# Forming the low parts of the first block's mixer weights with accumulating DMAs instead of VectorE subtractions

## The chip, the cores and the metric

The kernel runs on one core of a Trainium2 chip. The metric is the device time of one execution in microseconds (us). The kernel before takes 1753.9 us (median of three runs, 1749.92 to 1758.46).

## The reference

The reference is two transformer-like blocks on 512 tokens of width 1024, all in fp32. The first block (the one that the change touches) projects the modulated input `h` into its mixers and merges them:

```python
h = modulate(rmsnorm(x, norm1_g[i]), sh1, sc1)
q, k, v, hv, hx1, hx2, gna, ghy = jnp.split(h @ w_in[i], IN_SPLITS, axis=-1)
y_na = neighbourhood_attention(to_heads(q), to_heads(k), to_heads(v), to_heads(k_c), to_heads(v_c), na_rpb[i])
y_hy = hyena_mixer(hv, hx1, hx2, *hy_params)
x = x + g1 * gated_merge(gna, ghy, y_na, y_hy, w_na_o[i], w_hy_o[i], w_out[i])
```

`k_c` and `v_c` come from a second, 256-token context through `w_in`, the shift and scale `sh1`, `sc1` from a conditioning vector through `w_ada`, and the Hyena filters from a small network. Then come a SwiGLU layer, and the second block with three more mixers and a convolutional feed-forward layer. Nothing of these is changed.

## The kernel before

**How a product is computed.** Every large matrix product is done in three TensorE passes on the type fp32r, which holds a shortened fp32. A weight tile `w` is split into a high part `wh` (ScalarE's copy of `w` into fp32r, shown as CAST) and a low part `wl = w - wh` (VectorE's TENSOR_TENSOR, `lo`, line 778). `mm` (line 788) then adds `wh*xh + wh*xl + wl*xh` in one PSUM bank. The other operand `x` is split in the same way.

**How weights arrive.** `stream` (line 797) is a generator over weight groups of 128 x 1024 fp32 (512 KB, eight blocks of 128 x 128). For each it takes a buffer `raw`, loads it on SP's queue, takes `wh` and `wl`, and splits. The seven streams that the change touches are `w_hy` (12 groups, Hyena's input projection), `w_kvc` (4, the context's keys), `w_na` (12, attention's q, k and v), `w_gna` and `w_ghy` (8 each, the gates), `w_hyo` and `w_nao` (4 each, the output projections): 52 groups. All other streams, the modulation weights `w_ada` and the row-wise weights keep the subtraction.

**What sets the order.** No engine's order is written by hand. The program records every operation as a call, and `Trace.schedule` (line 542) simulates all engines with modelled durations and hand-over times (the tables `LAG`, `RELEASE` and the function `time`). It gives each engine the ready call of best rank, hands out SBUF space (48 segments named `pages`) and PSUM banks as it goes, and repeats forward and backward passes to improve the ranks (`plan`, line 691). `emit` (line 707) then issues the calls in the order of their planned starts from one line, 714; so every instruction of the trace carries that line, and tiles are told apart only by `pages`, `banks`, `small` or a name such as `mod`. Each engine works its own instructions strictly in this order and waits on semaphores. SP carries all DMAs of the kernel before; GpSimd (POOL) only clears padding.

**The start.** TensorE works first on the Hyena filters and on the modulation (`modulation_first`, line 1027: sixteen `w_ada` groups, each split and multiplied by the conditioning vector). Beside it VectorE and ScalarE compute the norm of `x`: squares, their sum, a reciprocal square root in a chain of small VectorE operations (tile `small`), a broadcast by TensorE, and then eight scaling operations that read `gs1` and eight that subtract the high part of `h` (they read `mod`). The first product of `h` with `w_hy` follows. From there on the filters, the context branch and the gates are woven between the products of the mixers.

Of the kernel before, what the change touches and what calls it, by code (L numbers as in the profile page):

```python
# [15 lines left out]
F32 = mybir.dt.float32  # L16
F32R = mybir.dt.float32r
I32 = mybir.dt.int32
BF16 = mybir.dt.bfloat16
AF = mybir.ActivationFunctionType  # L20
ALU = mybir.AluOpType
# [140 lines left out]
def layout(inp):  # L162
# [77 lines left out]

ENGINES = ("tensor", "vector", "scalar", "gpsimd", "sync")
PE, DVE, ACT, POOL, DMA = range(5)

LAG = (
    (0.0, 197.0, 197.0, 220.0, 1280.0),
    (152.0, 127.0, 128.0, 155.0, 1220.0),
    (108.0, 131.0, 150.0, 165.0, 1235.0),
    (75.0, 75.0, 75.0, 102.0, 1170.0),  # L250
    (1500.0, 2000.0, 1000.0, 1300.0, 2250.0),
)
APART = 0.7
ALONE = (DVE,)
DMA_START = 1700.0
RELEASE = 200.0, 150.0, 150.0, 100.0, 1200.0
TABLES = {AF.Silu: (0,), AF.Sin: (1, 0), AF.Exp: (2,), AF.Gelu_apprx_tanh: (3,)}
TABLE_LOAD = 1283.0
WEIGHTS = 13.3
# [203 lines left out]
class Trace:  # L463
    def __init__(self, nc, tc):
        self.nc, self.tc = nc, tc
        self.calls, self.lead, self.urgent = [], 0, False
        for i, name in enumerate(ENGINES):
            setattr(self, name, Engine(self, (i,)))
        self.either = Engine(self, (DVE, POOL))

    @contextmanager
# [6 lines left out]
    @staticmethod  # L478
    def time(engine, name, out, args, kw):

        n = out.free_size()
        if engine == PE:
            cols = args[1].ap.free_size()
            if name == "transpose":
                return max(2 * n / 2.4, 53)
            if args[1].ap.dtype == F32R:
                return max(n / 2.4 + WEIGHTS, cols / 1.2 + 5.0)
            return max(4 * n / 2.4 + 2.5, cols / 0.6 if n < 16 else cols / 0.3 if cols > 64 else 54)
        if engine == DVE:
            return (98 if name == "scalar_tensor_tensor" else 70) + 1.042 * n  # L490
        if engine == ACT:
            return 60 + 0.87 * n + (120 if name == "activation" and ("scale" in kw or "bias" in kw) else 0)
        if engine == POOL:
            return 150 + 2.1 * n
        return max(450.0, out.size() * 4 / 360.0)

    @staticmethod
    def shares_port(engine, name, reads, writes):
# [219 lines left out]
class Program:  # L718
# [75 lines left out]
        mm(out, wl, xh, start=False, stop=stop)  # L794
        self.pe += 3 * out.ap.free_size() / 2.4

    def stream(self, ap):

        for gi in range(ap.shape[0]):
            raw = self.u4()  # L800
            self.load(raw, ap[gi])
            wh, wl = self.u4(dt=F32R), self.u4(dt=F32R)
            self.split((wh, wl), raw)
            for j in range(8):
                yield wh[:, j * P : j * P + P], wl[:, j * P : j * P + P]

# [399 lines left out]
    def hyena(self):  # L1206
        nc, a = self.nc, self.a
        V = nc.vector
        blocks = self.stream(a["w_hy"])

        def conv_tile(m):
            ps = self.proj(blocks, self.h)
# [121 lines left out]
    def context(self):  # L1334

        nc = self.nc
        self.context_norm()
        yield
        blocks = self.stream(self.a["w_kvc"])
        self.kc, self.vc = [], []  # L1340
        for j in range(6):
            if j < 4:
                ps = self.proj(blocks, self.hc, 256)
            elif j == 4:
                out = self.proj_rows(self.a["w_vc"], self.hc)
            if j >= 4:
                t = self.u4(dt=F32R)
                self.vc.append(t)
                v, ps = t.rearrange("p (h z d) -> p h z d", z=2, d=64), out[j - 4].rearrange("p (h d) -> p h d", d=64)
                d = v[:, :, 0], v[:, :, 1]  # L1350
                nc.scalar.copy(d[0], ps)
                nc.vector.tensor_tensor(out=d[1], in0=ps, in1=d[0].bitcast(F32), op=ALU.subtract)
            else:
                self.kc.append(self.stacked_keys(ps, 256))
            yield
# [88 lines left out]
    def neighbourhood(self):  # L1444
        nc, a = self.nc, self.a
        V = nc.vector
        rope = self.u4()
        self.load(rope, a["rope1"])
        rc, rs = rope[:, :T], rope[:, T:]
        swap = [(i + 16) % 32 for i in range(32)]  # L1450
        blocks = self.stream(a["w_na"])
        self.y_na = []

        def rotate(x):
            sh, t1 = self.u2(), self.u2()
            V.stream_shuffle(sh, x, swap)
            nc.gpsimd.tensor_tensor(out=t1, in0=x, in1=rc, op=ALU.mult)
            V.tensor_tensor(out=sh, in0=sh, in1=rs, op=ALU.mult)
            V.tensor_tensor(out=t1, in0=t1, in1=sh, op=ALU.add)
            return t1  # L1460

        for hp in range(4):

            ps = self.proj(blocks, self.h)
            q = self.u2()
            nc.scalar.activation(q, ps, AF.Copy, scale=0.125)
            qp = self.stacked_queries(q)
            qr = self.stacked_queries(rotate(q))
            yield
            ps = self.proj(blocks, self.h)  # L1470
            k = self.u2()
            nc.scalar.copy(k, ps)
            kr = self.stacked_keys(rotate(k))
            yield
            ps = self.proj(blocks, self.h)
            v = self.u2()
            nc.scalar.copy(v, ps)
            vof = {}
            for off in ((0, 128, 256, 384), (64, 192, 320)):
                pt = self.psum("t")  # L1480
                n = len(off)
                for j, o in enumerate(off):
                    self.transpose(pt[:, j * P : j * P + P], v[:, o : o + P])
                t = self.u4(n * 256, F32R)
                to, ptv = t.rearrange("p (j h z d) -> p j h z d", h=2, z=2, d=64), pt[:, : n * P].rearrange("p (j h d) -> p j h d", h=2, d=64)
                for hd in range(2):
                    nc.scalar.copy(to[:, :, hd, 0], ptv[:, :, hd])
                    V.tensor_tensor(out=to[:, :, hd, 1], in0=ptv[:, :, hd], in1=to[:, :, hd, 0].bitcast(F32), op=ALU.subtract)
                vof.update((o, t[:, j * 256 : j * 256 + 256]) for j, o in enumerate(off))
            yield  # L1490
            o, sums = self.u2(), self.u0(8)
            for hd in range(2):
                bias = self.u4(768)
                self.load(bias, a["rpb"][2 * hp + hd])
                banks = []
                for b in range(4):
                    s = self.psum("s")
                    off = WIN_OFF[b]
                    kind = (0, 1, 1, 2)[b]
                    qsl = slice(b * P, b * P + P)  # L1500
                    self.scores(s[:, :256], hd, qr, qsl, kr, off)
                    self.scores(s[:, 256:], hd, qp, qsl, self.kc[hp], 0)
                    st = self.u0(6)
                    V.tensor_tensor_reduce(out=s[:, :256], in0=s[:, :256], in1=bias[:, kind * 256 : kind * 256 + 256], scale=1.0, scalar=-3e38, op0=ALU.add, op1=ALU.max, accum_out=st[:, 0:1])
                    V.reduce_max(out=st[:, 1:2], in_=s[:, 256:], axis=AX.X)
                    V.tensor_scalar(out=st[:, 2:3], in0=st[:, 0:1], scalar1=st[:, 1:2], scalar2=-1.0, op0=ALU.max, op1=ALU.mult)
                    pr = self.u2()
                    nc.scalar.activation(pr, s, AF.Exp, bias=st[:, 2:3], accum_out=sums[:, hd * 4 + b : hd * 4 + b + 1])
                    if b % 2 == 0:
                        banks.append(self.psum("o"))  # L1510
                    values = [vof[off + j * P][:, hd * P : hd * P + P] for j in range(2)]
                    values += [self.vc[j][:, (2 * hp + hd) * P : (2 * hp + hd) * P + P] for j in range(2)]
                    self.stacked_pv(banks[-1][:, b % 2 * 256 : b % 2 * 256 + 256], [pr[:, j * P : j * P + P] for j in range(4)], values)
                    yield
                self.summed_parts(o[hd * 64 : hd * 64 + 64], banks)
            d = self.over_sums(o, sums)
            self.y_na.append(d)
            yield
# [4 lines left out]

    def gate_na(self):

        blocks = self.stream(self.a["w_gna"])
        self.gna = self.scratch("gna")
        for m in range(KT):
            ps = self.proj(blocks, self.h)
# [5 lines left out]
    def branch_hy(self):  # L1535

        nc = self.nc
        gb, ob = self.stream(self.a["w_ghy"]), self.stream(self.a["w_hyo"])
        self.bhy = self.scratch("bhy")
        for m in range(0, KT, 2):  # L1540
            gs = []
# [11 lines left out]
    def merge1(self, mem):  # L1553
        nc, a = self.nc, self.a
        V = nc.vector
        ob = self.stream(a["w_nao"])
        nat = lambda x: x.rearrange("p (cb r c) -> p cb r c", r=8, cb=8)
        merged = []
        for m in range(KT):
            gb = self.u4()  # L1560
# [762 lines left out]
```

## Time and profile before

| | value |
|---|---|
| median of three runs | 1753.9 us |
| the profiled execution's own time | 1758.72 us |
| its span, first to last instruction | 1756.9 us |
| its mean granted TensorE clock | 0.993 of full speed |
| TensorE matmul busy | 1710.2 us, 97% |
| VectorE busy | 1194.7 us, 68% |
| ScalarE busy | 729.7 us, 42% |
| GpSimd busy | 29.2 us, 2% |
| DMA | 235.42 MB, mean 134 GB/s |

Busy time is what an engine spent in instructions that compute; waiting, semaphores and the issuing of DMAs are not in it. The granted clock is given as a share of full speed, 2.4 GHz; the lower of its two levels is 1.2 GHz, so 0.84 in a stretch says that about a third of that stretch ran at the lower level. The 40 slices of the page (44 us each) show how TensorE, VectorE and the DMA engines are loaded over the span: TensorE is below nine tenths in the first two slices alone, VectorE is at eight or nine tenths in the second to sixth, the tenth to thirteenth and the 28th to 31st.

### The profile page before, as it was taken

How to read it: one execution, taken by the hardware profiler on the slowest of the kernel's cores; microseconds unless marked ns; L12 is line 12 of the kernel's file. 1: busy time of each engine (PE TensorE's matmuls, PEld its weight loads, DVE VectorE, ACT ScalarE, POOL GpSimd, SP SyncE). 2: the span in 40 equal slices, each digit the busy share in tenths (PEclk: the TensorE clock that was granted, in tenths of full speed). 3: DMA queues.
4: the chain of work that ended last, by engine and by line, in shares of the span. 5: the costliest groups of instructions: out<-in, count | busy, mean ns of one | idle time of the engine just before them, and what ended most of it. 6: DMA issues, size and time to landing. Idle time of an engine off the chain costs nothing. (4 is left out here: it accounts for less than half of the span.)

```text
span 1756.9 us, 22940 instructions
## 1 busy us (share of the span) xinstructions
PE 1710.2 (97%) x8494; PEld 1416.4 (81%) x8494; DVE 1194.7 (68%) x2473; ACT 729.7 (42%) x1204; POOL 29.2 (2%) x69
## 2 busy tenths in 40 slices
PE   4799999999999999999999999999999999999999
PEld 3489988888888888888887887888877888888887
DVE  6999887759998266344377856659998635887520
ACT  5634345655554121233153431556564412454310
POOL 0000000000000000000000000010100000000000
PEclk9899999999999999999998999999999999999999
DMA  7644332427963324313254455412257221222420
GB/s 253 233 142 143 100 102 90 145 84 251 356 242 119 112 92 160 119 61 127 77 175 163 142 145 158 135 60 75 85 196 271 98 94 60 81 76 72 146 100 19
DMA packets 93662, 235.42 MB, mean 134 GB/s; under 512 B 18316, under 2 KB 26252, under 8 KB 93550
## 3 DMA queue, kind: packets, MB, share of 16 engines
q1 hardware_dynamic: 93550, 233.95, 39.2%
q8 instruction: 67, 1.10, 0.3%
q14 instruction: 45, 0.37, 0.1%
HBM read 206.91 MB, written 27.00 MB: 133 GB/s over the span
## 5 line engine op out<-in xcount | busy, mean ns | idle before, releaser
L714 PE MATMUL banks<-pages,pages 128*128 128x512 f32 (+5 forms) x7830 | 1663.5, 372 | 30.9 <-ACT pages L714 21.3
L714 PEld LDWEIGHTS banks<-pages,pages 128*128 128x128 f32 (+3 forms) x7830 | 1343.0, 185 | 305.8 <-ACT pages L714 25.3
L714 DVE TENSOR_TENSOR pages<-pages,pages 128x1024 fp32r<-128x1024 f32 (+12 forms) x747 | 616.7, 855 | 99.0 <-ACT pages L714 69.7
L714 ACT CAST pages<-pages 128x1024 fp32r<-128x1024 f32 (+4 forms) x471 | 396.9, 871 | 350.9 <-PE banks L714 111.6
L714 DVE TENSOR_TENSOR pages<-banks,pages 128x512 fp32r<-128x512 f32 (+7 forms) x219 | 111.8, 523 | 95.4 <-PE banks L714 73.4
L714 DVE TENSOR_TENSOR pages<-banks,R 128x512 f32<-128x512 f32 x81 | 57.0, 707 | 113.7 <-PE banks L714 113.6
L714 ACT ACTIVATE pages<-banks 128x512 f32<-128x512 f32 (+4 forms) x75 | 37.6, 512 | 227.8 <-PE banks L714 220.3
L714 DVE TENSOR_TENSOR pages<-pages,banks 128x512 f32<-128x512 f32 x66 | 43.9, 681 | 102.6 <-PE banks L714 85.7
L714 ACT ACTIVATE pages<-pages 128x512 f32<-128x512 f32 (+4 forms) x91 | 50.8, 571 | 148.0 <-DVE pages L714 138.8
L714 ACT COPY pages<-banks 128x512 f32<-128x512 f32 (+6 forms) x121 | 58.4, 502 | 96.1 <-PE banks L714 86.9
L714 ACT ACTIVATE pages<-pages,vec 128x512 f32<-128x512 f32 (+1 forms) x84 | 63.0, 768 | 63.7 <-DVE pages L714 53.1
L714 DVE SCALAR_TENSOR_TENSOR pages<-pages,vec,pages 128x511 f32<-128x511 f32 (+3 forms) x114 | 82.6, 745 | 3.3 <-ACT pages L714 2.6
L714 PE MATMUL banks<-ident,pages 128*128 128x128 f32 (+2 forms) x464 | 70.7, 273 | 7.2 <-issue 3.4
L714 PEld LDWEIGHTS banks<-ident,pages 128*128 128x128 f32 (+2 forms) x464 | 55.2, 144 | 21.4 <-ACT pages L714 8.8
L714 ACT CAST pages<-banks 128x512 fp32r<-128x512 f32 (+5 forms) x118 | 53.6, 472 | 26.1 <-PE banks L714 19.6
L714 ACT ACTIVATE pages<-banks,small 128x512 f32<-128x512 f32 (+3 forms) x80 | 46.6, 588 | 28.3 <-DVE small L714 27.4
L714 POOL MEMSET pages<- 128x1 f32 (+4 forms) x63 | 28.6, 475 | 1220.7 <-DVE pages L714 713.8
L714 DVE SCALAR_TENSOR_TENSOR pages<-pages,pages 128x1024 bf16<-128x1024 f32 (+3 forms) x42 | 42.9, 1021 | 1.6 <-DMA gna<-pages 1.4
L714 DVE SCALAR_TENSOR_TENSOR pages<-banks,mod,pages 128x512 f32<-128x512 f32 x16 | 11.7, 745 | 43.1 <-PE banks L714 43.1
L714 DVE SCALAR_TENSOR_TENSOR pages<-pages,banks 128x512 f32<-128x512 f32 x40 | 27.1, 682 | 6.0 <-PE banks L714 6.0
L714 DVE TENSOR_TENSOR pages<-pages 128x16 f32<-128x16 f32 (+6 forms) x107 | 29.3, 308 | 1.8 <-DMA pages<-in_eye_dram 1.5
L714 DVE TENSOR_REDUCE small<-banks 128x1 f32<-128x256 f32 (+3 forms) x64 | 27.9, 447 | 0.3
(73 smaller groups left out, 384.1 us busy)
## 6 DMA issues: line engine op xcount, KB each, us to landing
pages<-in_w_f_dram SPq DMA_DIRECT2D x66, 512.0 KB, 3.8
pages<-in_w_ada_dram SPq DMA_DIRECT2D x48, 512.0 KB, 6.5
pages<-in_w_up_dram SPq DMA_DIRECT2D x44, 512.0 KB, 3.2
pages<-in_w_g_dram SPq DMA_DIRECT2D x24, 512.0 KB, 4.0
pages<-in_w_down_dram SPq DMA_DIRECT2D x22, 512.0 KB, 4.0
pages<-in_w_out_dram SPq DMA_DIRECT2D x16, 512.0 KB, 7.8
pages<-in_w_hy_dram SPq DMA_DIRECT2D x12, 512.0 KB, 5.0
pages<-in_w_na_dram SPq DMA_DIRECT2D x12, 512.0 KB, 3.4
```

What stands on the lines that cost most here:

```text
L714: self.tc.keep_in_program_order(f(*map(at, c.args), **{k: at(v) for k, v in c.kw.items()}))
```

## The change

`stream` gets a flag `dma`, set for the seven streams named above. With it VectorE's subtraction goes. In its place ScalarE writes `-wh` into `wl` (an ACTIVATE with scale -1), and a DMA issued by GpSimd reads the weight group a second time from HBM and adds it to what stands in `wl`. The planner gets a sixth resource, `SUM`, for these DMAs, with its own hand-over times and an assumed rate; `SUM` calls are issued on GpSimd's queue, in one line with its MEMSETs.

```diff
-ENGINES = ("tensor", "vector", "scalar", "gpsimd", "sync")
-PE, DVE, ACT, POOL, DMA = range(5)
+ENGINES = ("tensor", "vector", "scalar", "gpsimd", "sync", "gpsimd")
+PE, DVE, ACT, POOL, DMA, SUM = range(6)
 LAG = (
-    (0.0, 197.0, 197.0, 220.0, 1280.0),
+    (0.0, 197.0, 197.0, 220.0, 1280.0, 1500.0),
...
+    (3000.0, 3000.0, 3000.0, 3000.0, 3000.0, 3000.0),
 )
+SUM_RATE = 200.0
-        return max(450.0, out.size() * 4 / 360.0)
+        return max(450.0, out.size() * 4 / (SUM_RATE if engine == SUM else 360.0))
-    def stream(self, ap):
+    def stream(self, ap, dma=False):
         for gi in range(ap.shape[0]):
             raw = self.u4()
             self.load(raw, ap[gi])
             wh, wl = self.u4(dt=F32R), self.u4(dt=F32R)
-            self.split((wh, wl), raw)
+            if dma:
+                self.nc.scalar.copy(wh, raw)
+                self.nc.scalar.activation(wl, wh.bitcast(F32), AF.Copy, scale=-1.0)
+                self.nc.sums.dma_start(out=wl, in_=ap[gi].bitcast(F32R), accum_op=ALU.add)
+            else:
+                self.split((wh, wl), raw)
-        blocks = self.stream(a["w_hy"])
+        blocks = self.stream(a["w_hy"], True)
```

The same flag is set where `w_kvc`, `w_na`, `w_gna`, `w_ghy`, `w_hyo` and `w_nao` are streamed. Since the planner decides anew, the whole order of every engine changes. Two places are shown (numbers behind `pages` tell buffers apart; they are not the same buffers in the two kernels).

VectorE, before, at the end of the reciprocal square root (`small`) up to the first operations that scale `x` (they read `gs1`):

```order
L714 TENSOR_TENSOR small0_64<-small0_64 128x4
L714 TENSOR_TENSOR pages43_587<-pages11_568,pages29_203 128x512
L714 SCALAR_TENSOR_TENSOR small0_64<-small0_64 128x4
L714 SCALAR_TENSOR_TENSOR pages16_155<-banks0_65,pages16_155 1x512
L714 SCALAR_TENSOR_TENSOR gs1_74<-mod_73,vec_66 128x8
L714 SCALAR_TENSOR_TENSOR small0_64<-small0_64 128x4
L714 TENSOR_TENSOR pages46_471<-pages12_466,pages44_481 128x1024
L714 TENSOR_TENSOR pages11_568<-pages40_556,banks0_65 128x512
L714 TENSOR_TENSOR pages10_435<-pages40_556,banks0_65 128x512
L714 SCALAR_TENSOR_TENSOR pages41_446<-pages21_175,gs1_74,banks0_65 128x512 x2
```

VectorE, in the changed kernel, at the same place:

```order
L717 TENSOR_TENSOR small0_64<-small0_64 128x4
L717 TENSOR_TENSOR mod_73<-pages19_165,vec_66 128x8
L717 TENSOR_TENSOR pages10_356<-pages44_242,pages0_63 128x512
L717 SCALAR_TENSOR_TENSOR small0_64<-small0_64 128x4
L717 TENSOR_TENSOR mod_73<-mod_73,pages19_165 128x8
L717 TENSOR_TENSOR pages24_188<-pages47_424,pages12_262 128x512
L717 SCALAR_TENSOR_TENSOR small0_64<-small0_64 128x4
L717 SCALAR_TENSOR_TENSOR gs1_74<-mod_73,vec_66 128x8
L717 SCALAR_TENSOR_TENSOR pages40_563<-banks0_65,pages16_155 1x512
L717 TENSOR_TENSOR pages47_424<-pages28_201,banks0_65 128x512
L717 SCALAR_TENSOR_TENSOR pages7_603<-pages21_175,gs1_74,banks0_65 128x512 x2
```

The 128x1024 subtraction of a `w_hy` group (`pages46_471`) that stood between the last `small` and the first `gs1` operation is gone, and the last two operations that make `mod` now stand later in the chain.

TensorE, before, at the first products of `h` with `w_hy`:

```order
L714 MATMUL banks0_65<-pages22_179,pages34_469 128x512 [waits Activation_49]
L714 MATMUL banks0_65<-pages22_179,pages44_481 128x512 [waits DVE_49]
L714 MATMUL banks0_65<-pages20_632,pages34_469 128x512 [waits DVE_49]
L714 MATMUL banks0_65<-pages22_179,pages36_534 128x512
L714 MATMUL banks0_65<-pages29_203,pages34_469 128x512 [waits Activation_49]
L714 MATMUL banks0_65<-pages20_632,pages44_481 128x512
```

TensorE, in the changed kernel, at the same place (`DMASW` is a semaphore of the DMAs that GpSimd issues):

```order
L717 MATMUL banks0_65<-pages24_188,pages38_469 128x512 [waits Activation_49]
L717 MATMUL banks0_65<-pages24_188,pages30_484 128x512 [waits DVE_49]
L717 MATMUL banks0_65<-pages45_434,pages38_469 128x512 [waits DVE_49]
L717 MATMUL banks0_65<-pages24_188,pages11_441 128x512 [waits DMASW0_49]
L717 MATMUL banks0_65<-pages29_203,pages38_469 128x512 [waits Activation_49]
```

The first matmul that reads a low part (`pages11_441`) now waits for an accumulating DMA, where before it (`pages36_534`) needed a VectorE result.

## Rows read from the trace of the kernel before

**Rows 1.** The page's head: span, and busy time of each engine.

```profile
span 1756.9 us, 22940 instructions
PE 1710.2 (97%) x8494; PEld 1416.4 (81%) x8494; DVE 1194.7 (68%) x2473; ACT 729.7 (42%) x1204; POOL 29.2 (2%) x69
```

**Rows 2.** Waits of TensorE, whole span: us in total, times, longest us.

```profile
PE banks L714 <- ACT pages L714: 26.3, 12, 9.9
PE banks L714 <- DVE pages L714: 8.9, 6, 3.7
PE banks L714 <- issue: 3.4, 1, 3.4
PE banks L714 <- DMA pages<-in_hy_mlp_dram: 3.2, 1, 3.2
```

**Rows 3.** Waits of TensorE from 0 to 50 us.

```profile
PE banks L714 <- ACT pages L714: 20.0, 3, 9.9
...
PE banks L714 <- DVE pages L714: 0.3, 1, 0.3
```

**Rows 4.** Waits of TensorE from 50 to 100 us.

```profile
PE banks L714 <- DVE pages L714: 4.0, 3, 1.8
...
PE banks L714 <- ACT pages L714: 2.0, 2, 1.2
```

**Rows 5.** Matmuls by shape, 400 to 500 us (count, busy us, mean ns).

```profile
L714 PE MATMUL banks<-pages,pages 128*128 128x512 f32 x368 | 89.3, 393 | 0.0
```

**Rows 6.** The same, 700 to 800 us.

```profile
L714 PE MATMUL banks<-pages,pages 128*128 128x512 f32 x435 | 99.9, 390 | 0.0
```

**Rows 7.** Windows: length, busy (instructions) of each engine, clock, DMA share, GB/s.

```profile
48.00:61.00 13.00, 7.32 (x32) 2.42 (x32) 11.30 (x13) 7.17 (x10) 0.00 (x0) 0.86 0.95 342
61.00:72.50 11.50, 10.33 (x43) 4.04 (x42) 11.17 (x19) 8.19 (x14) 0.00 (x0) 0.87 0.89 309
72.50:83.00 10.50, 9.64 (x42) 7.45 (x41) 8.93 (x23) 6.00 (x13) 0.00 (x0) 0.84 0.37 131
83.00:100.00 17.00, 14.87 (x61) 11.06 (x62) 17.00 (x26) 7.53 (x13) 0.00 (x0) 1.00 0.20 54
...
160.00:180.00 20.00, 20.00 (x109) 17.34 (x108) 20.00 (x28) 7.03 (x10) 0.33 (x4) 1.00 0.55 182
...
450.00:500.00 50.00, 50.00 (x246) 41.92 (x245) 48.16 (x98) 19.99 (x33) 0.00 (x0) 1.00 0.95 353
```

**Rows 8.** VectorE by shape, whole span (count, busy us, mean ns).

```profile
L714 DVE TENSOR_TENSOR pages<-pages,pages 128x1024 fp32r<-128x1024 f32 x289 | 349.2, 1217 | 64.4 <-ACT pages L714 45.5 <-issue 9.7 <-PE banks L714 8.4
...
L714 DVE TENSOR_TENSOR pages<-pages,pages 128x512 fp32r<-128x512 f32 x123 | 81.4, 684 | 12.3 <-ACT pages L714 5.6 <-PE banks L714 4.1 <-issue 2.1
```

**Rows 9.** ScalarE by shape, whole span.

```profile
L714 ACT CAST pages<-pages 128x1024 fp32r<-128x1024 f32 x289 | 298.7, 1047 | 252.0 <-PE banks L714 104.2 <-DMA pages<-in_w_down_dram 30.4 <-DMA pages<-in_w_f_dram 22.5
```

**Rows 10.** VectorE in order of time: start, us, operation.

```profile
67.84 0.16 DVE L714 TENSOR_SCALAR small<-banks 128x4 f32<-128x4 f32 x1
...
78.13 1.21 DVE L714 TENSOR_TENSOR pages<-pages,pages 128x1024 fp32r<-128x1024 f32 x1
...
81.41 2.06 DVE L714 SCALAR_TENSOR_TENSOR pages<-pages,gs,banks 128x512 f32<-128x512 f32 x3
```

**Rows 11.** TensorE in order of time.

```profile
87.47 13.75 PE L714 MATMUL banks<-pages,pages 128*128 128x512 f32 x57 [1.64 <-DVE pages L714]
```

**Rows 12.** DMA issues: count, KB each, median us from issue to landing.

```profile
pages<-in_w_hy_dram SPq DMA_DIRECT2D x12, 512.0 KB, 5.0
...
pages<-in_w_nao_dram SPq DMA_DIRECT2D x4, 512.0 KB, 4.5
...
pages<-in_decay_dram SPq DMA_DIRECT2D x2, 512.0 KB, 10.4
```

More of the change, by code (lines that the diff above doesn't have):

```diff
@@ L237, in layout @@
     return {k: np.ascontiguousarray(v) for k, v in a.items()}
-ENGINES = ("tensor", "vector", "scalar", "gpsimd", "sync")
-PE, DVE, ACT, POOL, DMA = range(5)
+ENGINES = ("tensor", "vector", "scalar", "gpsimd", "sync", "gpsimd")
+PE, DVE, ACT, POOL, DMA, SUM = range(6)
 LAG = (
-    (0.0, 197.0, 197.0, 220.0, 1280.0),
[L248 to L251, printed above, removed]
+    (0.0, 197.0, 197.0, 220.0, 1280.0, 1500.0),
+    (152.0, 127.0, 128.0, 155.0, 1220.0, 1500.0),
+    (108.0, 131.0, 150.0, 165.0, 1235.0, 1500.0),
+    (75.0, 75.0, 75.0, 102.0, 1170.0, 1500.0),
+    (1500.0, 2000.0, 1000.0, 1300.0, 2250.0, 2500.0),
+    (3000.0, 3000.0, 3000.0, 3000.0, 3000.0, 3000.0),
 )
@@ L255 @@
 DMA_START = 1700.0
-RELEASE = 200.0, 150.0, 150.0, 100.0, 1200.0
+RELEASE = 200.0, 150.0, 150.0, 100.0, 1200.0, 1200.0
+SUM_RATE = 200.0
 TABLES = {AF.Silu: (0,), AF.Sin: (1, 0), AF.Exp: (2,), AF.Gelu_apprx_tanh: (3,)}
@@ L466, in __init__ @@
         self.calls, self.lead, self.urgent = [], 0, False
-        for i, name in enumerate(ENGINES):
+        for i, name in enumerate(ENGINES[:SUM]):
             setattr(self, name, Engine(self, (i,)))
+        self.sums = Engine(self, (SUM,))
         self.either = Engine(self, (DVE, POOL))
@@ L1338, in context @@
         yield
-        blocks = self.stream(self.a["w_kvc"])
+        blocks = self.stream(self.a["w_kvc"], True)
         self.kc, self.vc = [], []
@@ L1450, in neighbourhood @@
         swap = [(i + 16) % 32 for i in range(32)]
-        blocks = self.stream(a["w_na"])
+        blocks = self.stream(a["w_na"], True)
         self.y_na = []
@@ L1524, in gate_na @@
     def gate_na(self):
-        blocks = self.stream(self.a["w_gna"])
+        blocks = self.stream(self.a["w_gna"], True)
         self.gna = self.scratch("gna")
@@ L1537, in branch_hy @@
         nc = self.nc
-        gb, ob = self.stream(self.a["w_ghy"]), self.stream(self.a["w_hyo"])
+        gb, ob = self.stream(self.a["w_ghy"], True), self.stream(self.a["w_hyo"], True)
         self.bhy = self.scratch("bhy")
@@ L1555, in merge1 @@
         V = nc.vector
-        ob = self.stream(a["w_nao"])
+        ob = self.stream(a["w_nao"], True)
         nat = lambda x: x.rearrange("p (cb r c) -> p cb r c", r=8, cb=8)
```

## The prediction, written before the run

> **What bounds the kernel now.** I read the page's head first, then TensorE's waits for the whole span and by stretch, then its matmuls by shape in two stages, and last the windows of the start. The head shows TensorE busy for 1710.2 of 1756.9 us [rows 1], so at most 46.7 us can be had from waiting. The list of its waits names 26.3 + 8.9 + 3.4 + 3.2 = 41.8 us of them [rows 2]. They are early. The single waits for a first load (3.2 us) and for no named engine (3.4 us) lie before 50 us and between 50 and 100 us. With them, 20.0 + 3.2 + 0.3 = 23.5 us lie before 50 us [rows 2, 3], 4.0 + 3.4 + 2.0 = 9.4 us between 50 and 100 us [rows 2, 4], and 41.8 - 23.5 - 9.4 = 8.9 us are left for the other 1650 us.
>
> Busy is not yet at its peak, so I compare the pace. From 700 to 800 us TensorE runs 435 wide matmuls and next to nothing else [rows 6]: 100 / 435 = 0.23 us for one. From 400 to 500 us, in the mixers, it runs 368 [rows 5]; these need 368 x 0.23 = 84.6 us, and the rest goes to narrower ones. VectorE is busy 48.16 of 50 us in that stage [rows 7], and TensorE still holds its pace. From 100 us on VectorE is full but TensorE does not wait for it. What the change can move by more than a few us is therefore the start, up to 87.47 us, where TensorE's last wait of that stage ends [rows 11], and whatever new wait it makes later.
>
> **The change part by part.** It takes 52 subtractions (seven streams, 12 + 4 + 12 + 8 + 8 + 4 + 4 groups) of 1.217 us [rows 8] off VectorE, 63.3 us in all. It adds 52 negations on ScalarE and 52 DMAs on GpSimd's queue, which read 52 x 0.524 = 27.3 MB from HBM once more.
>
> *Before the first product of `h`.* I counted VectorE's order ahead of the first operation that reads `gs1`: before, 23 operations of 128x1024 and 48 that are 512 wide; now 21 and 47. Two `w_hy` subtractions have gone (one is the 1.21 us at 78.13 us, between the root's chain that starts at 67.84 us and the scaling at 81.41 us [rows 10]) and one narrower operation. That is 2 x 1.217 + 0.684 = 3.1 us [rows 8]. Between 48 and 83 us VectorE is busy 11.30 + 11.17 + 8.93 = 31.4 of 35 us [rows 7], so what leaves it there shortens the start nearly in full: -3.1 us. The lower bound is no gain, if the `w_ada` loads set that time (the DMA engines are at 0.95 and 0.89 there [rows 7]); the other bound is rival A.
>
> *The other 50 subtractions*, 60.8 us, I put at 0: TensorE's own work covers them, as its pace shows. If that cover were gone, one could come late by 1.2 us.
>
> *The negations.* The nearest row is the CAST of the same shape, 1.047 us [rows 9]: 52 x 1.05 = 55 us more on ScalarE. Five stand ahead of the first operations that make `h`. ScalarE is busy 7.17 + 8.19 + 6.00 = 21.4 of 35 us there [rows 7], so five more fit beside: 0. One stands between the two copies of a modulation row and could delay the second, +1.05 us at most.
>
> *The adds.* No row shows an accumulating DMA. From below it is a plain load of 512 KB: 4.5 us [rows 12]. From above it is twice the slowest load in the table, 2 x 10.4 = 20.8 us, since it has the weights and `wl` to read. I take twice the usual load, 2 x 5.0 = 10 us [rows 12], nearest to the row of the same tiles. Against that stands the lead that the new order gives. Counted in the built program, 52 to 233 matmuls stand between an add and the first matmul that reads its result, in the middle 140. The middle case (98 wide, 42 half as wide) is 98 x 0.23 + 42 x 0.115 = 27 us. The tightest four have 52, 69, 70 and 74; the tightest is a `w_na` group with 30 wide and 22 narrower, 30 x 0.23 + 22 x 0.115 = 9.4 us. At 10 us one add is late by 0.6 us: +0.6 us.
>
> *What is queued behind.* TensorE has 52 new waits for adds, and since it works in order all its work stands behind each. SP, which carries every load, has 38 waits for an add whose page it reuses; a late add delays all loads behind it. GpSimd's MEMSETs now stand behind adds, but the nearest reader of one is 137 matmuls away, at least 137 x 0.115 = 16 us: 0. The DMA engines get 27.3 MB more in the first 560 us or so; where they are full, 450 to 500 us [rows 7], only a few of the adds fall, and they fit in the lead.
>
> *The later waits*, 8.9 us, depend on an order that is planned anew: 0, with 3 us either way.
>
> The sum is -3.1 + 0.6 = -2.5 us. The profiled execution took 1758.72 us, its span and 1.8 us around it, so 1756.2 us in its terms. That run is 4.8 us above the median of 1753.9 us, so I take the difference off the median: 1751.4 us.
>
> **Rivals.** *A: the whole start closes up.* VectorE's relief lets the modulation and the filters move up as well, so that TensorE's 9.4 us of waits between 50 and 100 us go [rows 2, 4] and the granted clock stays at its upper level. Between 48 and 83 us it was 0.86, 0.87 and 0.84 [rows 7], which cost 7.32 x 0.14 + 10.33 x 0.13 + 9.64 x 0.16 = 3.9 us. That gives 1753.9 - 13.3 = 1740.6 us. For it speaks that VectorE is the fullest engine there; against it, that the DMA engines are full in the same stretch, that 3.4 us of the waits name no engine at all, and that the adds bring new load just then.
>
> *B: the adds come late, and TensorE waits for them.* Place: the waits on GpSimd's DMA semaphores, first at the tight groups. It decides from 9.4 us per add, and at about 18.5 us it costs (18.5 - 9.4) + (18.5 - 69 x 0.23) = 11.7 us and outweighs the gain by 0.5%. At the upper bound of 20.8 us it costs 11.4 at the tightest and 4.9 at the start, some 16.3 us: 1753.9 - 3.1 + 16.3 = 1767 us. An add that is not slow itself can be held up: if GpSimd could prepare adds only in VectorE's pauses, those from 160 to 180 us, where VectorE is busy 20.00 of 20 us [rows 7], would wait for 20 us and more, with a price of the same size. The Trainium skill states such a lock (SBUF — State Buffer, the section on the memory's doors): a DMA issued from GpSimd has its descriptors written by that engine, which is shut out while VectorE runs in a two-port mode. It excepts `tensor_tensor`, which is nearly all of VectorE's work here (its section Who interferes with whom infers that exception), and no run here shows either; by it the hold-ups stay as short as one narrow operation and my sum stands. For B speaks that add, semaphore and page hand-back have no row at all; against it, the leads of 27 us.
>
> *C: the change takes work from an engine that gates nothing.* The planner fills VectorE's freed time with filter work, the `w_ada` loads set the start, and the time stays at 1753.9 us, or moves by the 3 us of a new order. For it speaks that 48 of 50 subtractions were covered anyway; against it, the row count ahead of `gs1`.
>
> **How the numbers follow.** My forecast gets 0.57, with a range of its own from 1747 to 1758 us (no gain and 4 us of new waits at one end, the 3.1 us and half as much again at the other). A gets 0.13, B 0.16, C 0.14. About 0.5%, 8.8 us, is what a measurement of this kernel can tell from no change. A alone is faster by more: 0.13. B alone is slower by more: 0.16. The rest is within: 0.71. The range of 1742 to 1766 us holds the forecast and C and reaches to within 2 us of A and B, so that about half of each lies in it. The predicted time is the forecast's, 1751.4 us.
>
> **What would show it.** Right: from 100 us on TensorE's waits stay under some 12 us and its count in the 400 to 500 us window does not fall; VectorE's busy time falls by about 63 us and ScalarE's rises by about 55; the steady run of matmuls starts about 3 us before 87.47 us; TensorE waits for accumulating DMAs for 1 us or less. A would show as a clock of 1.00 from 48 to 83 us and a steady start at about 74 us. B would show as TensorE waiting for DMAs on `w_hy` and `w_na`, with GpSimd's adds landing 18 us or more after issue. C would show as a steady start still at 87 us. I am wrong if the difference arises after 100 us, on either side.

## The result, and the profile after

The changed kernel takes 1775.38 us (median of four runs, 1770.28 to 1777.84), the kernel before 1753.6 us (four runs): a ratio of 1.0119, 95% interval 1.0085 to 1.0152. It is slower by 1.2%, and lies outside the range of 1742 to 1766 us. The profiled execution took 1775.97 us.

The head of the page after answers to [rows 1]:

```profile
span 1774.1 us, 23092 instructions
PE 1710.9 (96%) x8494; PEld 1417.4 (80%) x8494; DVE 1140.7 (64%) x2421; ACT 774.3 (44%) x1253; POOL 74.1 (4%) x121
```

The span grew by 17.2 us and TensorE's busy time by 0.7 us, so the rest is idle TensorE. Its waits over the whole span (us in total, times, longest), against [rows 2]:

```profile
PE banks L717 <- ACT pages L717: 28.4, 13, 10.0
PE banks L717 <- DVE pages L717: 24.7, 16, 7.5
PE banks L717 <- DMA pages<-in_hy_mlp_dram: 3.5, 1, 3.5
PE banks L717 <- DMA pages<-s5g: 1.4, 1, 1.4
PE banks L717 <- DVE small L717: 0.4, 1, 0.4
```

The sum is 58.4 us, against 41.8. The same view from 0 to 50 us adds up to 22.3 us (23.5 before) and from 50 to 100 us to 10.2 us (9.4 before). That leaves 25.9 us after 100 us, where there were 8.9. None of them names an accumulating DMA. Of the 17.0 us more, 13.4 are waits for VectorE (18.0 us after 100 us, against 4.6). Windows with all engines, of the changed kernel, against [rows 7] (length, busy and count of TensorE, its weight loads, VectorE, ScalarE and GpSimd, granted clock, DMA share, GB/s):

```profile
48.00:61.00 13.00, 7.58 (x32) 2.50 (x30) 12.12 (x16) 9.07 (x13) 0.00 (x0) 0.87 0.92 323
61.00:72.50 11.50, 11.50 (x52) 5.84 (x51) 11.24 (x24) 8.66 (x13) 2.75 (x3) 0.85 0.80 205
72.50:83.00 10.50, 7.25 (x32) 5.41 (x32) 6.90 (x15) 8.03 (x13) 1.73 (x2) 0.93 1.05 316
83.00:100.00 17.00, 15.51 (x60) 12.39 (x61) 16.76 (x37) 8.90 (x19) 0.18 (x1) 0.84 0.72 199
450.00:500.00 50.00, 42.10 (x205) 34.86 (x204) 38.11 (x71) 24.16 (x43) 2.60 (x3) 0.90 1.01 339
```

From 72.5 to 83 us the DMA share went from 0.37 to 1.05, and from 83 to 100 us from 0.20 to 0.72. At 450 to 500 us TensorE, which never stopped before, is busy for 42.10 of 50 us, and its clock is 0.90. From 400 to 500 us it runs 282 wide matmuls, not 368 [rows 5]:

```profile
L717 PE MATMUL banks<-pages,pages 128*128 128x512 f32 x282 | 72.4, 402 | 1.2 <-DVE pages L717 1.2
```

The largest wait and VectorE's idle time behind it stand in the timelines of TensorE and VectorE (start, us, operation, idle time before it and what ended it):

```profile
475.13 1.65 PE L717 MATMUL banks<-pages,pages 128*128 128x256 f32 x5 [7.51 <-DVE pages L717]
```

```profile
473.72 0.43 DVE L717 TENSOR_TENSOR pages<-pages,pages 128x256 f32<-128x256 f32 x1 [9.83 <-DMA bhy<-pages]
```

VectorE stands idle for 9.83 us until a store of `bhy` has landed, with the evictions that TensorE needs queued behind it. At that place `gna` and `bhy`, which were put off to DRAM, are loaded back, and SP issues these loads and the store in one line (timeline of SP):

```profile
458.14 0.32 SPq L717 DMA_DIRECT2D pages<-bhy  x1
461.41 0.32 SPq L717 DMA_DIRECT2D pages<-gna  x1
465.49 0.32 SPq L717 DMA_DIRECT2D pages<-bhy  x1
466.07 0.32 SPq L717 DMA_DIRECT2D bhy<-pages  x1
```

The gaps of some 3 and 4 us between them are SP's waits for earlier transfers to land (from 455 to 468 us):

```profile
SPq L717 <- DMA pages<-bhy: 4.0, 2, 3.7
SPq L717 <- DMA pages<-in_w_out_dram: 3.4, 1, 3.4
SPq L717 <- DMA pages<-gna: 3.4, 3, 2.9
```

So the store is issued late, at 466.07 us, and is slow itself: VectorE goes on 7.65 us after it. The DMA issues from 440 to 475 us (count, KB each, median us from issue to landing) show that the reloads and the stores are slow there, and `w_nao`'s adds beside them (GpSimd issues these, shown as POOLq):

```profile
pages<-in_w_nao_dram POOLq DMA_DIRECT2D x4, 512.0 KB, 9.4
pages<-gna SPq DMA_DIRECT2D x8, 256.0 KB, 11.3
pages<-bhy SPq DMA_DIRECT2D x7, 256.0 KB, 15.4
...
bhy<-pages SPq DMA_DIRECT2D x2, 256.0 KB, 7.6
```

In the same window of the kernel before:

```profile
pages<-gna SPq DMA_DIRECT2D x8, 256.0 KB, 4.6
pages<-bhy SPq DMA_DIRECT2D x8, 256.0 KB, 4.7
...
bhy<-pages SPq DMA_DIRECT2D x2, 256.0 KB, 3.6
```

Not every load is slower: those of `w_ada` land after 5.6 us there, where it was 9.4 us before. What the 52 adds cost the 16 DMA engines stands in the page's queue table of the changed kernel (queue: packets, MB, share of the span):

```profile
q1 hardware_dynamic: 93550, 233.95, 39.0%
q0 software_dynamic: 7488, 27.27, 8.5%
```

A plain MB takes 0.390 x 1774 / 233.95 = 3.0 us of all 16 engines, an added one 0.085 x 1774 / 27.27 = 5.5 us. The share adds up the packets' time and can pass 1 (1.05 above), so this is a price by that count and not a strict occupancy.

### The profile page after: what moved, and what is told of

Its sections match the earlier page's. It is cut to its first block, busy times and chain, and to the rows that moved or that the text cites. A ratio compares the mean times of both kernels' runs of the same rounds, so it can differ in the third digit from the quotient of the medians.

```text
span 1774.1 us, 23092 instructions
## 1 busy us (share of the span) xinstructions
PE 1710.9 (96%) x8494; PEld 1417.4 (80%) x8494; DVE 1140.7 (64%) x2421; ACT 774.3 (44%) x1253; POOL 74.1 (4%) x121
## 3 DMA queue, kind: packets, MB, share of 16 engines
q1 hardware_dynamic: 93550, 233.95, 39.0%
q0 software_dynamic: 7488, 27.27, 8.5%
## 4 chain that ended last, share of the span: by engine, by line
PE 72%; DVE 5%; DMA 5%; ACT 2%; issue 1%; SPq 1%; ACTq 0%; DVEq 0%
PE banks L717 72%; DVE pages L717 4%; ACT pages L717 2%; DMA pages<-gna 1%; DMA bhy<-pages 1%; DMA pages<-in_w_out_dram 1%; DMA gna<-pages 1%; SPq L717 1%; DVE small L717 1%; DMA pages<-in_w_ada_dram 1%; DMA pages<-in_w_g_dram 1%; DMA br<-pages 0%; DVE banks L717 0%; DMA pages<-s5g 0%; DMA pages<-bhy 0%
## 5 line engine op out<-in xcount | busy, mean ns | idle before, releaser
L717 PE MATMUL banks<-pages,pages 128*128 128x512 f32 (+8 forms) x7830 | 1664.5, 372 | 46.4 <-DVE pages L717 24.7
L717 DVE TENSOR_TENSOR pages<-pages,pages 128x1024 fp32r<-128x1024 f32 (+11 forms) x695 | 553.0, 825 | 126.9 <-ACT pages L717 91.5
L717 ACT ACTIVATE pages<-pages 128x512 f32<-128x512 f32 (+5 forms) x143 | 105.2, 748 | 152.5 <-DVE pages L717 151.8
L717 ACT COPY pages<-banks 128x512 f32<-128x512 f32 (+5 forms) x121 | 58.4, 501 | 79.8 <-PE banks L717 78.5
L717 DVE SCALAR_TENSOR_TENSOR pages<-pages,vec,pages 128x511 f32<-128x511 f32 (+3 forms) x120 | 87.3, 747 | 6.3 <-ACT pages L717 4.8
L717 ACT CAST pages<-banks 128x512 fp32r<-128x512 f32 (+5 forms) x118 | 53.4, 474 | 12.8 <-PE banks L717 10.2
L717 ACT ACTIVATE pages<-banks,small 128x512 f32<-128x512 f32 (+3 forms) x80 | 46.5, 588 | 22.3 <-DVE small L717 18.8
L717 DVE TENSOR_TENSOR pages<-pages 128x16 f32<-128x16 f32 (+7 forms) x107 | 31.6, 331 | 0.6
```

The costliest lines, as they stand in the source:

```text
L717: self.tc.keep_in_program_order(f(*map(at, c.args), **{k: at(v) for k, v in c.kw.items()}))
```

## The experiments

In the code, `...` stands for lines left out. Theory 1 is that the adds' transfers do the harm: they fill the DMA engines and so make other loads late. Theory 2 is that the planner's new order does it. Kernels with the same instructions in the same order were compared matmul by matmul: "x us later" is the difference of the starts of the same one of the 8494 matmuls.

**Adds of 8 KB.**

```diff
+            if c.engine == SUM:
+                self.tc.keep_in_program_order(f(out=at(c.kw["out"])[:, :16], in_=c.kw["in_"][:, :16], accum_op=ALU.add))
+                continue
...
-                self.nc.scalar.activation(wl, wh.bitcast(F32), AF.Copy, scale=-1.0)
+                self.nc.scalar.activation(wl, wh.bitcast(F32), AF.Copy, scale=-1e-4)
```

> The changed kernel with every instruction in its place, but each of the 52 accumulating DMAs moves 16 of the 1024 columns (8 KB instead of 512 KB), and the negation writes a ten-thousandth of the hi part instead of its whole, so the numbers stay tame; most of each lo part is left out of the computation. Theory 1 (the transfers: 27 MB more on the DMA engines, at a poor rate, make the reloads of gna and bhy late at 440 to 480 us and the other holes after 100 us): TensorE's waits after 100 us fall from 25.9 to 9 us or less, the 7.5 us hole near 475 us goes, and the time is 1751 us (1747 to 1756), 24 us under the changed kernel. Theory 2 (the order: the planner counts the adds as an engine of their own, and places stores and loads on SP where they hold each other up): the hole stays, SP still waits some 20 us for VectorE before a store of bhy near 400 us, and the time is 1772 us (1766 to 1778).

It took 1754.65 us, ratio to before 1.0007 (0.9994 to 1.0020). The loss is gone with the bytes, although the order is that of the changed kernel to the last instruction; SP's wait before the store of `bhy` is still 18.8 us. TensorE has no wait left from 440 to 480 us; after 100 us its waits are 12.1 us, more than the 9 us that theory 1 had foreseen. Theory 2 falls as the only cause.

One thing in theory 1 needs care. All engines from 440 to 480 us, of the changed kernel and of this one:

```profile
440.00:480.00 40.00, 31.81 (x185) 27.11 (x184) 27.74 (x64) 26.38 (x53) 3.46 (x4) 0.88 0.96 290
```

```profile
440.00:480.00 40.00, 39.93 (x208) 33.48 (x207) 38.91 (x73) 24.94 (x43) 2.60 (x3) 1.00 1.04 387
```

The DMA engines are as full without the bytes (1.04): from 440 to 475 us they carry 13 loads of `w_ada`, where the changed kernel has 3. But the reloads land after 5.5 us (`gna`) and 6.1 us (`bhy`), and TensorE loses nothing. So a full share alone does no harm; reloads that land late do, and they came with the adds' bytes.

Against this kernel, the profiled changed kernel is 4.4 us later at 100 us, 8.8 at 380, 10.3 at 450, 21.1 at 500 and 19.3 at the end.

**The same transfers added to the kernel before.** Each reads the same 512 KB and adds them to its own part of a DRAM tensor, behind the subtraction (`extra` holds the subtractions of the seven streams):

```diff
+            if c.number in self.extra:
...
+                self.tc.keep_in_program_order(self.nc.gpsimd.tensor_copy(self.spot[:, i : i + 1], at(wl).bitcast(F32)[:, :1]))
+                self.tc.keep_in_program_order(self.nc.gpsimd.dma_start(out=self.heap[:, i * 1024 : i * 1024 + 1024], in_=w, accum_op=ALU.add))
```

> The kernel before with every instruction in its place and VectorE's subtractions kept; behind each of the 52 subtractions GpSimd copies one column of the lo part (so that it waits for it) and then issues an accumulating DMA of the same 512 KB of weights into DRAM that nothing reads. No instruction of the kernel waits for these. Theory 1 (the transfers themselves): the same bytes late the same loads; TensorE's waits after 100 us rise from 8.9 to 20 us or more, and the time is 1768 us (1762 to 1778). Theory 2 (the order of the changed kernel): nothing that the kernel waits for is moved, the waits stay at 9 us, and the time is 1754 us (1750 to 1758).

It took 1774.29 us, 1.0120 (1.0097 to 1.0143): the whole loss of the change, with the order and the subtractions of before and no instruction of the kernel waiting for an add. The place is another one (from 410 to 500 us the matmuls fall from 5.1 to 19.0 us behind the first profile of before), and part of it is there at 100 us: 2.8 us against the first profile of before, 6.8 against the second one below. By its queue table an add costs 0.088 x 1775 / 27.27 = 5.7 us per MB here, close to the 5.5, but its target is DRAM and its places are others. That the two kernels lose the same to 1 us is therefore in part luck. The window of TensorE alone from 400 to 440 us in this kernel:

```profile
400.00:440.00 40.00, 33.88 (x167) 0.98 0.90 279
```

In the kernel before (all engines):

```profile
400.00:440.00 40.00, 40.00 (x204) 33.62 (x203) 36.65 (x71) 24.21 (x46) 0.00 (x0) 1.00 0.70 245
```

**Plain writes in place of the adds.**

```diff
+            if c.engine == SUM:
+                c.kw.pop("accum_op")
```

> The changed kernel with every instruction in its place, but GpSimd's 52 DMAs write the weights instead of adding them, so each lo part is the whole weight and the mixer's weights count double. As many bytes are moved from HBM; nothing is read back and added. Theory 1a (an added byte costs the DMA engines 5.5 us per MB where a plain one costs 3.0, and that is what hurts): 27.26 MB then cost 82 instead of 150 us of the 16 engines, and the time falls by more than half of the 21 us: 1758 us (1753 to 1765). Theory 1b (the bytes and the places of the transfers hurt whatever their kind): 1772 us (1767 to 1777).

It took 1759.28 us, 1.0023 (1.0011 to 1.0036). The queue table of this kernel:

```profile
q1 hardware_dynamic: 93550, 233.95, 39.9%
q0 software_dynamic: 7488, 27.27, 4.8%
```

The same 27.27 MB now take 0.048 x 1755 / 27.27 = 3.1 us per MB. Packet by packet the traces say the same: the median packet of 4 KB on GpSimd's queue takes 0.328 us as an add and 0.174 us as a plain write. By the medians 16.1 of the 20.7 us that the bytes cost are gone. So it is the price of adding, more than the second reading of the weights, that does the harm. What is left falls at 450 to 500 us: this kernel is 0.7 us behind the one with adds of 8 KB until 450 us and 4.9 at 500.

**w_nao's four adds, and the 48 others.** Two kernels, each with one part cut to 8 KB. The first is shown; the second has `!=` in place of `==` and the two scales exchanged:

```diff
+            if c.engine == SUM and c.kw["in_"].tensor.name == "in_w_nao_dram":
+                self.tc.keep_in_program_order(f(out=at(c.kw["out"])[:, :16], in_=c.kw["in_"][:, :16], accum_op=ALU.add))
+                continue
...
-                self.nc.scalar.activation(wl, wh.bitcast(F32), AF.Copy, scale=-1.0)
+                self.nc.scalar.activation(wl, wh.bitcast(F32), AF.Copy, scale=-1e-4 if ap.tensor.name == "in_w_nao_dram" else -1.0)
```

> The changed kernel with every instruction in its place, but the four adds for w_nao alone (issued at 448 to 463 us) move 8 KB instead of 512 KB, and most of these lo parts is left out. Theory A (these four transfers, among the reloads of gna and bhy, make the 11 us that are lost at 460 to 470 us): the 7.5 us hole goes and the time is 1764 us (1760 to 1768). Theory B (the store of bhy for which SP waits 20 us near 400 us holds back the loads behind it, and these crowd the stretch whatever the four adds do; or the delays before 440 us are what comes due): the hole keeps 4 us or more, and the time is 1772 us (1768 to 1777).

> The changed kernel with every instruction in its place; the four adds for w_nao are whole, the 48 others move 8 KB each (most of their lo parts is left out): the other half of the kernel in which w_nao's alone were cut, which took 1764.8 us. Theory A (the four adds make the loss at 455 to 475 us by themselves, whatever came before): the hole of 7 us stands, and the time is 1765 us (1761 to 1768), 10 over the kernel with all 52 cut. Theory B (they only bring due what the earlier adds have delayed): the hole is under 2 us and the time is 1756 us (1752 to 1759).

Without `w_nao`'s bytes it took 1764.84 us, 1.0049 (1.0030 to 1.0067); with them alone 1765.43 us, 1.0055 (1.0038 to 1.0073). Theory A holds in both as to the time, and the two parts add up: 10.2 + 10.8 = 21.0 us over the 1754.65. Four adds of 512 KB cost as much as the other 48. The DMA issues from 440 to 475 us without their bytes:

```profile
pages<-gna SPq DMA_DIRECT2D x8, 256.0 KB, 5.8
pages<-bhy SPq DMA_DIRECT2D x8, 256.0 KB, 6.2
```

and with their bytes alone:

```profile
pages<-gna SPq DMA_DIRECT2D x8, 256.0 KB, 9.6
pages<-bhy SPq DMA_DIRECT2D x8, 256.0 KB, 10.6
```

The form was not as theory A had it: with these bytes alone there is no single hole of 7 us, but several waits of TensorE of 1.3 to 2.0 us (timeline of TensorE, 440 to 480 us):

```profile
449.63 4.62 PE L720 MATMUL banks<-pages,pages 128*128 128x256 f32 x18 [2.00 <-DVE pages L720]
...
466.80 4.62 PE L720 MATMUL banks<-pages,pages 128*128 128x256 f32 x21 [1.50 <-DVE pages L720]
```

**Only the 16 adds of w_hy and w_kvc**, whole, and then cut to 8 KB as above. `w_gna`, `w_ghy`, `w_hyo` and `w_nao` are changed as `w_na` is here:

```diff
-        blocks = self.stream(a["w_na"], True)
+        blocks = self.stream(a["w_na"])
```

> The accumulating DMAs for w_hy and w_kvc alone (16 of the 52, all issued before some 190 us); the other five streams keep VectorE's subtraction, and the planner orders the whole anew. Both theories: the start keeps its 3 us. Theory 1: with no add at 200 to 480 us the reloads of gna and bhy land as before (about 4.7 us), no wait over 2 us stands at 440 to 480 us, and the time is 1751 us (1747 to 1756). Theory 2: any new order may hold a store ahead of loads; 1751 us if this one does not, up to 1765 us if it does, and then SP shows a wait of 10 us or more for VectorE while the DMA engines stand idle.

> The kernel with adds for w_hy and w_kvc alone, every instruction in its place, but these 16 adds move 8 KB each and most of these lo parts is left out. It took 1764.7 us with the whole adds, 10 us over the kernel before, which neither theory had foreseen. Theory 1 (the transfers again, at 60 to 200 us this time, where the trace shows the 10 us lost): 1754 us (1749 to 1757). Theory 2 (the new order of that kernel): 1764 us (1761 to 1768).

With whole adds it took 1764.67 us, 1.0075 (1.0055 to 1.0095), which theory 1 had not foreseen: I had taken 440 to 480 us for the one sensitive place. Theory 2 had allowed up to 1765 us. Nor did the start keep its 3 us, as both theories had it: the steady run starts at 88.76 us. With adds of 8 KB in the same order it took 1753.89 us, 0.9998 (0.9986 to 1.0011). So it is the bytes here too: with them the matmuls are 5.4 us later at 100 us and 9.5 at 200. TensorE's windows from 100 to 200 us, with whole adds and with small ones:

```profile
100.00:200.00 100.00, 96.38 (x580) 1.00 0.75 200
```

```profile
100.00:200.00 100.00, 99.63 (x613) 1.00 0.45 142
```

**A planner that counts the adds.** Each occupies the planner's DMA resource for twice a load's time and is usable 4.5 us later:

```diff
+SUM_LAG = 4500.0
...
+        c.sum = engines == (SUM,)
+        if c.sum:
+            engines = (DMA,)
...
+        c.time = [self.time(e, name, big, args, kw) * (2 if c.sum else 1) for e in engines]
...
+                        if (d if back else c).sum:
+                            gap += SUM_LAG
...
+            f = getattr(self.nc.gpsimd if c.sum else getattr(self.nc, ENGINES[c.engine]), c.name)
```

> All 52 accumulating DMAs as in the changed kernel, but the planner counts each as an occupant of its DMA resource for 2.9 us (twice a plain load's) and as usable 4.5 us later than it does for a plain load; GpSimd still issues them. Theory 1: the bytes stay, the order can only spread them; TensorE's waits after 100 us fall from 25.9 to 12 to 20 us, and the time is 1763 us (1756 to 1772). Theory 2: with the order right the waits are back at 9 us and the time is 1751 us (1747 to 1756).

It took 1756.43 us, 1.0016 (1.0007 to 1.0026), at the low end of theory 1's range and just above theory 2's, which ended at 1756. TensorE's waits after 100 us are 15.4 us, as theory 1 had them (12 to 20). All 27.27 MB are still added. TensorE's windows of this kernel:

```profile
400.00:440.00 40.00, 38.40 (x209) 1.00 0.96 276
440.00:500.00 60.00, 59.17 (x296) 1.00 0.99 341
```

The DMA share from 400 to 440 us is 0.96, where the changed kernel had 0.70. The transfers were moved ahead (`w_nao`'s adds are issued at 427.9 to 445.4 us, in the changed kernel at 447.9 to 462.8), and 19 of the 21 us are back. So both theories hold a part: the bytes do the harm, in an order that was planned as if they cost the DMA engines nothing.

**Six adds at the start, with that planner.** The flag of `w_hy` becomes 6 (groups below it are added), the other streams lose theirs.

> Accumulating DMAs for the first six groups of w_hy alone, those that were issued before TensorE's steady run in the kernel with the retimed planner, with that planner; the other 46 groups keep VectorE's subtraction. Theory 1: VectorE has the start's subtractions off it, six adds of 512 KB take some 16 us of the DMA engines between 60 and 90 us, and nothing stands later: steady run 4 to 5 us earlier and 1750 us (1746 to 1755). Theory 2 (any new order costs some us later, bytes or none): 1755 us (1752 to 1762).

It took 1757.16 us, 1.0010 (0.9998 to 1.0022). Theory 1's 1750 us did not come; theory 2's range holds it. The steady run starts at 83.98 us, no earlier than in the second execution of the kernel before (83.44, below). Nothing here beats the kernel before.

**bhy's stores on GpSimd's queue.**

```diff
+            if c.engine == DMA and getattr(getattr(c.kw["out"], "piece", None), "name", "") == "bhy":
+                f = self.nc.gpsimd.dma_start
```

> The changed kernel with every instruction in its place among the others, but the eight stores of bhy are issued by GpSimd instead of SP, so that no load on SP stands behind a store that waits 20 us for VectorE near 400 us. Theory A (the hole at 460 to 470 us is made by the four adds for w_nao among the reloads, and the held queue has no part in it): 1775 us (1771 to 1779). Theory B (the held loads crowd the stretch after 420 us, and the adds do harm only in that crowd): the DMA engines are busy at 405 to 418 us, the hole shrinks by 5 us or more, and the time is 1767 us (1762 to 1771).

It took 1778.09 us, 1.0139 (1.0119 to 1.0158), which lies in theory A's range. But it tells nothing of theory B, since SP's queue was not freed: its waits from 395 to 480 us now hold one of 27.1 us for the next thing in its order, a page that TensorE still reads.

```profile
SPq L719 <- PE banks L719: 44.7, 10, 27.1
```

**Second traces of both kernels, unchanged.**

> The kernel before once more, unchanged, for a second trace of its start. Theory S1 (the profiled execution of before, 4.7 us over the median, had a slow start, so that a typical one is already as far as the changed order without its bytes): this execution takes some 1752 to 1756 us and its TensorE is 2 to 5 us ahead of the first profile's at 100 us. Theory S2 (the start is the same in every execution and the spread comes later): within 1 us of the first profile at 100 us.

> The changed kernel once more, unchanged, for a second trace. If the losses are places of the program they stand again: some 2 us at 240 to 260 us, 3 to 4 us at 330 to 440 us and 8 us or more at 455 to 475 us, and the time is 1770 to 1778 us; if they are accidents of one execution, they move or go.

The second execution of before took 1750.16 us. From 90 to 400 us every matmul of it is 4.0 us ahead of the first profile, and the steady run of [rows 11] starts so much earlier without any change:

```profile
83.44 13.75 PE L714 MATMUL banks<-pages,pages 128*128 128x512 f32 x57 [1.62 <-DVE pages L714]
```

So the start that S1 foresaw came, though not its time (1752 to 1756 us). Which start is the usual one two traces cannot say: the first execution lies 4.8 us over the median of 1753.9, the second 3.7 us under it. The second one of the changed kernel took 1774.95 us. Against adds of 8 KB it is 2.6 us later at 100 us, 8.8 at 410 to 450 and 19.6 at 500; TensorE again waits 7.00 us for VectorE near 473 us. The large loss is a place of the program. The smaller ones are less so: against adds of 8 KB the first profile loses 1.7 us from 200 to 260 us and 1.5 from 380 to 410, the second one 0.6 and 4.1.

## Why the prediction was wrong

*What bounds the kernel*: TensorE, as forecast. Its busy time moved by 0.7 us, and the loss is its waits (58.4 - 41.8 = 16.6 of the 17.2 us); its clock fell at 80 to 88 and in 450 to 500 us too, but it falls in places of the kernel before as well [rows 7], and on balance little of that is left in the busy time. One reading of the rows was too strong: from 100 us on VectorE is not full throughout (36.65 of 40 us from 400 to 440 us, 11.70 of 20 from 240 to 260 us in the kernel before).

*The start, -3.1 us*: it came in the row and not in the time. The steady run starts at 84.49 us in the changed kernel:

```profile
84.49 15.67 PE L717 MATMUL banks<-pages,pages 128*128 128x512 f32 x59 [3.33 <-DVE pages L717]
```

That is 3.0 us before 87.47 [rows 11]. But the second execution of before starts at 83.44 us, so the row I subtracted from moves by 4.0 us without any change; one execution does not carry a term of 3 us there. And the start that I had won was filled with the adds' transfers. Windows of the changed kernel:

```profile
80.00:84.00 4.00, 0.50 (x1) 0.19 (x1) 1.07 (x3) 3.85 (x7) 0.86 (x1) 0.69 1.08 354
84.00:88.00 4.00, 3.51 (x8) 2.56 (x9) 4.00 (x7) 1.19 (x2) 0.00 (x0) 0.50 1.02 206
```

and of the kernel with adds of 8 KB:

```profile
80.00:84.00 4.00, 3.14 (x12) 2.32 (x13) 4.00 (x7) 2.14 (x4) 0.00 (x0) 1.00 0.02 4
84.00:88.00 4.00, 4.00 (x19) 3.23 (x18) 4.00 (x7) 0.00 (x0) 0.00 (x0) 1.00 0.15 56
```

TensorE waits for VectorE here, and VectorE for a store of `spec` (a tensor that SP puts off to DRAM and loads back) to land:

```profile
83.03 1.41 DVE L717 SCALAR_TENSOR_TENSOR pages<-pages,gs,banks 128x512 f32<-128x512 f32 x2 [2.93 <-DMA spec<-pages]
```

So TensorE does 0.50 us of work in four, at a granted clock of 0.69, and the next four are granted the lower level, 0.50; without the bytes it runs on at 1.00. The order without its bytes takes the time of before (1754.65 us), the "no gain" that I had set as the lower bound. That is not proof that the relief is worth nothing: its steady run starts at 81.36 us, 2.1 us ahead of the second execution of before, but its waits after 100 us are 12.1 us against 8.9. What the start gained there, the new order may have lost later; no run separates the two.

*The other 50 subtractions at 0, the negations at 0*: right as far as the runs show, since the kernel with all of them and no bytes takes the time of before. The subtractions' group fell by 349.2 - 286.3 = 62.9 us, from [rows 8], as 63.3 us had been forecast; the 52 ACTIVATEs are the 55 us expected:

```profile
L717 DVE TENSOR_TENSOR pages<-pages,pages 128x1024 fp32r<-128x1024 f32 x237 | 286.3, 1218 | 77.1 <-ACT pages L717 71.4 <-PE banks L717 4.3 <-issue 1.0
...
L717 ACT ACTIVATE pages<-pages 128x1024 fp32r<-128x1024 f32 x52 | 55.0, 1062 | 0.6
```

The engines' busy times moved less, by -54.0 and +44.6 us, since busy time counts an overlap of two instructions once. Added up one by one, VectorE's instructions fell by 62.5 us and ScalarE's rose by 51.3 us, with three table loads fewer (3.9 us).

*The adds, +0.6 us*: the latency was right and the price was not in it. Of GpSimd's DMAs the trace gives:

```profile
DMA to landing us min/median/max: 5.2/7.8/11.2
```

I had taken 10 us, and TensorE waited for none. Rival B, which names TensorE's waits for adds, is therefore not what happened, though it had the sign. Rival A did not come either: the clock was 0.87, 0.85 and 0.93 from 48 to 83 us. Nor did VectorE hold GpSimd up: three adds were issued between 240 and 260 us, where VectorE is busy for 20.00 of 20 us, in 0.86 us each.

```profile
240.00:260.00 20.00, 18.34 (x91) 15.21 (x90) 20.00 (x27) 10.40 (x15) 3.12 (x4) 1.00 0.82 204
```

VectorE ran only TENSOR_TENSOR there. That agrees with the exception for `tensor_tensor` that the Trainium skill makes (SBUF — State Buffer, the section Who interferes with whom). Over the whole kernel before, `tensor_tensor` is 923.9 of the 1351.8 us of VectorE's instructions, added up one by one, less than the "nearly all" of the prediction.

*The step that failed* is the last sentence of "What is queued behind": "The DMA engines get 27.3 MB more in the first 560 us or so; where they are full, 450 to 500 us [rows 7], only a few of the adds fall, and they fit in the lead." The few are four, and they do fit in their own lead. But I asked only whether an add reaches its own reader in time, and not what it does to the transfers beside it. At 5.5 us per MB the four take 2.10 x 5.5 = 11.5 us of engines whose share was 0.95 already [rows 7], and the kernel with these four alone loses 10.8 us. That these two figures are close is luck as far as the runs show: the 48 others take 25.2 x 5.5 = 139 us by the same count and cost 10.2 us. What the runs show is the path: reloads of `gna` that land after 11.3 us instead of 4.6, a store of `bhy` behind them, VectorE idle for 9.83 us, TensorE for 7.51 us. With it falls "the later waits, 0, with 3 us either way": they grew by 17.0 us, and the sign that I had named for being wrong came: the waits grew after 100 us. (The lower end of the forecast's own range, 1747 us, does not come out of its terms either: 1753.9 less 3.1 and half as much again is 1749.2; nothing hung on it.) The Trainium skill says (DMA: Bandwidth & Descriptors, the section Issuing engines are not separate DMA queues) that DMAs of every issuing engine run on the same 16 DMA engines and interleave. The runs agree: with `w_nao`'s adds on GpSimd's queue cut, SP's reloads of `gna` land after 5.8 us, with them whole after 11.3.

What stays open: how the loss of the 48 other adds divides among the start and the places from 200 to 410 us differs between the two executions (4.4 and 2.6 us at 100 us, 10.3 and 8.8 at 450). Whether SP's wait near 400 us makes the crowd after it worse was not shown; in the kernel with adds of 8 KB it stands (18.8 us) and nothing is lost. Nor was it shown how the adds' packets hold up the reloads, since the engines' share is about 1 with and without them.

## What to carry to other kernels

Work moved from an engine to a DMA is paid for in the DMA engines' time of the stretch where it lands: work it out there, in engine time per MB of that kind of DMA, and ask which other transfer becomes late, not only whether the new one is in time. An accumulating DMA cost nearly twice a plain one here (5.5 against 3.1 us per MB). A DMA share near 1 is not itself a loss: look at when the transfers land that an engine waits for. Before you subtract from a single row of a start, look at a second execution; and when a planner orders the work, give it the resource that the new operation really uses.

## What was not expected of the hardware

- Accumulating DMAs of 512 KB from HBM into SBUF took 5.5 us of the 16 DMA engines per MB, where plain ones at the same places took 3.1; the issue of one on GpSimd took 0.865 us in the median, of a plain one 0.530.
- In the changed kernel TensorE was busy for 0.50 us from 80 to 84 us, at a granted clock of 0.69, and had 0.50 from 84 to 88; in its second execution it was busy for 2.01 us, at 0.57, and then had 0.58. In the second execution of the kernel before it was busy for 2.23 us, at 1.00, and kept 1.00.
- Two executions of the same program differ by 4.0 us at the start and by another 5.7 us between 800 and 1000 us, with every instruction in the same order.
